# Loads of a Winograd-style 3x3 convolution: from casting transfers on GpSimd's queue to fp32 transfers on SyncE's

## The chip, the cores and the metric

One core of one Trainium2 chip runs the whole kernel. The time of a run is the device time of that core in microseconds (us). The profile is one further execution, recorded instruction by instruction; its span is counted from its first to its last recorded event and is a little shorter than the time of the same execution.

The engines are called by the names of the profile: PE (TensorE, matrix multiplications; PEld is its loading of weights), DVE (VectorE), ACT (ScalarE), POOL (GpSimd) and SP (SyncE, which only issues transfers). Engines run their own instruction lists in order and wait for one another by semaphores. Transfers (DMAs) are issued from the list of SP, ACT or POOL, each with a queue of its own (q1 for SP, q10 for ACT, q0 for POOL), and all queues are served by the same 16 DMA engines.

## The reference

```python
def setup_inputs():
    batch, c_in, h, w, c_out = 16, 64, 64, 64, 128
    return {
        "x": np.random.randn(batch, c_in, h, w).astype(np.float32),
        "weight": np.random.randn(c_out, c_in, 3, 3).astype(np.float32) * 0.1,
    }

def reference(x, weight):
    x_pad = np.pad(x, ((0, 0), (0, 0), (1, 1), (1, 1)), mode='constant')
    output = np.zeros((batch, c_out, h, w), dtype=np.float32)
    ...
    output[b, co] += weight[co, ci, kh, kw] * x_pad[b, ci, kh:kh+h, kw:kw+w]
    ...
```

A 3x3 convolution with zero padding over 16 images of 64 channels and 64x64 points, giving 128 channels. In fp32, 16.8 MB come in and 33.6 MB go out.

## The kernel before

**Tiling.** Two images make a pair: 2 x 64 channels fill the 128 partitions, so one pair is a tile of 128 x (64x64), 16 KB per partition in fp32, 2.10 MB in all. There are NP = 8 pairs. Each pair is worked in four blocks of RB = 8 pairs of output rows (16 output rows).

**The arithmetic.** Vertically the kernel computes two output rows at once with a scheme in the manner of Winograd's. For each pair p it keeps the input in fp16 (`xs[p]`) and the sums of neighbouring rows in fp16 (`ss[p]`, half as many rows, made by `sums`). A block has three groups of matmuls, each into two PSUM tiles `acc` (one for each image of the pair): U from `ss` with the middle weight row (6 matmuls), A from `xs` (12) and Bt from `xs` (12). ACT copies U out of PSUM into `ut`; DVE then adds A and `ut` into the even output rows and Bt and `ut` into the odd ones (the two `tensor_add` on `ots`). PSUM has 8 `acc` tiles (banks), `ut` has 4.

**Loads.** SP's queue brings the weights and then pairs 0, 1 and 2 in fp32 (`x0`, `x1`, `x2`) into homes of the output pool. Their fp16 form is made by ACT and POOL (`cast`): pair 0 partly ahead of the loop; pairs 1 and 2 by ACT in pieces of 16 rows, placed by the table `later` behind the U copies of blocks of pairs 0 and 1. Pairs 3 to 7 come through POOL's queue, and the transfer itself turns fp32 into fp16 (`load`), straight into `xs`; pairs 6 and 7 come in two halves. POOL also makes the row sums of pair p+1 during pair p.

**Stores.** Output homes hold one image each (16 KB per partition, `opool`, seven of them, three of which first hold x0 to x2). Image 0 of a pair is stored by SP at the pair's end, image 1 is put on the list `held` and stored by ACT behind the next U copies. The last pair is stored in halves, at blocks 1 and 3; image 0 of the first pair too.

**Order.** `keep` holds instructions of one engine in the order in which the program names them; everything else follows the program's order by tile dependencies.

Of the kernel before, what the change touches and what calls it, by code (L numbers as in the profile page):

```python
# [8 lines left out]
F32 = mybir.dt.float32  # L9
F16 = mybir.dt.float16  # L10
# [3 lines left out]
def kernel(  # L14
# [6 lines left out]
    nc = tc.nc  # L21
    B, CI, H, W = x.shape
    CO = weight.shape[0]
    assert H == 64 and W == 64 and CI == 64 and CO == 128 and B % 2 == 0
    NP = B // 2
    RB = 8

    keep = tc.keep_in_program_order
    x_rows = x.rearrange("b c h w -> (b c) h w")
    out_rows = out.rearrange("b co h w -> b co h w")  # L30
    w_flat = weight.rearrange("co ci kh kw -> co (ci kh kw)")

    const = ctx.enter_context(tc.tile_pool(name="const", bufs=1))
    psum = ctx.enter_context(tc.tile_pool(name="psum", bufs=8, space=bass.MemoryType.PSUM))
    xpool = ctx.enter_context(tc.tile_pool(name="xpool", bufs=8))
    opool = ctx.enter_context(tc.tile_pool(name="opool", bufs=7))
    spool = ctx.enter_context(tc.tile_pool(name="spool", bufs=3))
    upool = ctx.enter_context(tc.tile_pool(name="upool", bufs=4))

    w_raw = const.tile([CO, CI * 9], F32)  # L40
    nc.sync.dma_start(w_raw, w_flat)
    x0 = opool.tile([128, H, W], F32, tag="ot", name="x0")
    nc.sync.dma_start(x0, x_rows[0:128, :, :])
    x1 = opool.tile([128, H, W], F32, tag="ot", name="x1")
    nc.sync.dma_start(x1, x_rows[128:256, :, :])
    x2 = opool.tile([128, H, W], F32, tag="ot", name="x2")
    nc.sync.dma_start(x2, x_rows[256:384, :, :])
    raws = {1: x1, 2: x2}
    ident = const.tile([128, 128], F16)
    make_identity(nc, ident)  # L50
    w16 = const.tile([CO, CI * 9], F16)
    keep(nc.gpsimd.tensor_copy(w16, w_raw))  # L52

    xs = {p: xpool.tile([128, H, W], F16, tag="xs", name="xs") for p in range(3)}

    def load(p, rows):
        xs[p] = xpool.tile([128, H, W], F16, tag="xs", name="xs")
        for lo in range(0, H, rows):
            keep(
                nc.gpsimd.dma_start(  # L60
                    xs[p][:, lo : lo + rows, :],
                    x_rows[128 * p : 128 * p + 128, lo : lo + rows, :],
                )
            )

    ss = {}

    def sums(eng, p, src, lo, n):
        if p not in ss:
            ss[p] = spool.tile([128, H // 2, W], F16, tag="ss", name="ss")  # L70
        v = src.rearrange("p (j i) c -> p j i c", i=2)
        keep(
            eng.tensor_add(  # L73
                ss[p][:, lo : lo + n, :], v[:, lo : lo + n, 0, :], v[:, lo : lo + n, 1, :]
            )
        )
# [5 lines left out]
    def wrow(i):  # L82
        return Wt[:, i, :, :].rearrange("p t c -> p (t c)")

    wps = {}
    for kh in (1, 2, 0):
# [3 lines left out]
            for q in (0, 64):  # L90
                nc.tensor.matmul(wp[q : q + 64, k * CO : k * CO + CO], w16[:, t::9], ident)  # L91
        wps[kh] = wp[:, 0 : 3 * CO]
    blank = const.tile([128, 400], F32)
    keep(nc.vector.memset(blank, 0.0))  # L94
    warm = psum.tile([128, 512], F32, tag="acc", name="warm")
    for _ in range(3):
# [3 lines left out]
    keep(nc.vector.tensor_sub(wrow(G21), wps[2], wrow(G1)))  # L100
    keep(nc.vector.tensor_sub(wrow(G01), wps[0], wrow(G1)))  # L101

    def cast(copy, p, src, lo, hi):
        keep(copy(xs[p][:, lo:hi, :], src[:, lo:hi, :]))  # L104

    for lo in (RB, 2 * RB, 3 * RB):
        sums(nc.vector, 0, x0, lo, RB)
    cast(nc.scalar.copy, 0, x0, 0, 18)
    keep(nc.scalar.copy(wrow(G0), wps[0]))  # L109
    keep(nc.scalar.copy(wrow(G2), wps[2]))  # L110
    cast(nc.gpsimd.tensor_copy, 0, x0, 34, 50)
    cast(nc.gpsimd.tensor_copy, 0, x0, 50, 64)
    for p in (3, 4):
        load(p, H)
    later = {
        (0, 0): [(0, x0, 18, 34)],
        (0, 2): [(1, x1, 0, 16), (1, x1, 16, 32)],
        (0, 3): [(1, x1, 32, 48), (1, x1, 48, 64)],
    }
    later.update({(1, n): [(2, x2, 16 * n, 16 * n + 16)] for n in range(4)})  # L120

    held = []

    whole = {3: (0, 64)}
    halves = {1: (0, 32), 3: (32, 64)}
    cuts_of = [(halves, whole)] + [(whole, whole)] * (NP - 2) + [(halves, halves)]

    def store(eng, p, b2, ot, lo, hi):
        return eng.dma_start(
            out_rows[2 * p + b2, :, lo:hi, :],  # L130
            ot.rearrange("p j i c -> p (j i) c")[:, lo:hi, :],
        )

    for p in range(NP):
        if p + 1 < NP:
            for lo in (0, 16):
                sums(nc.gpsimd, p + 1, raws.get(p + 1, xs[p + 1]), lo, 16)
                if (p, lo) == (1, 16):
                    for q in range(5, NP):
                        load(q, H if q == 5 else H // 2)  # L140
        ots = [
            opool.tile([128, H // 2, 2, W], F32, tag="ot", name="ot") for _ in range(2)
        ]
        for blk in range(4):
            j0 = blk * RB

            def group(wi_rows):

                tiles = [
                    psum.tile([128, RB, W], F32, tag="acc", name="acc") for _ in range(2)  # L150
                ]
                n = 3 * len(wi_rows)
                i = 0
                for wi, off in wi_rows:
                    for kw in (1, 0, 2):
                        c_lo, c_hi = max(0, 1 - kw), min(W, W + 1 - kw)
                        for b2 in range(2):
                            p0 = 64 * b2
                            lo, hi = j0, j0 + RB
                            if off is None:  # L160
                                rhs = ss[p][p0 : p0 + 64, lo:hi, c_lo + kw - 1 : c_hi + kw - 1]
                            else:
                                while 2 * lo + off < 0:
                                    lo += 1
                                while 2 * (hi - 1) + off > H - 1:
                                    hi -= 1
                                first = 2 * lo + off
                                last = 2 * (hi - 1) + off
                                rhs = xs[p][
                                    p0 : p0 + 64,  # L170
                                    first : last + 1 : 2,
                                    c_lo + kw - 1 : c_hi + kw - 1,
                                ]
                            nc.tensor.matmul(  # L174
                                tiles[b2][:, lo - j0 : hi - j0, c_lo:c_hi],
                                Wt[p0 : p0 + 64, wi, kw, :],
                                rhs,
                                start=i == 0,
                                stop=i == n - 1,
                            )  # L180
                        i += 1
                return tiles

            U = group([(G1, None)])
            us = []
            for b2 in range(2):
                ut = upool.tile([128, RB, W], F32, tag="ut", name="ut")
                keep(nc.scalar.copy(ut, U[b2]))  # L188
                us.append(ut)
            while held and (p, blk) != (1, 0):  # L190
                keep(store(nc.scalar, *held.pop(0)))
            for piece in later.get((p, blk), ()):
                cast(nc.scalar.copy, *piece)
            A = group([(G21, 1), (G0, -1)])
            for b2 in range(2):
                nc.vector.tensor_add(ots[b2][:, j0 : j0 + RB, 0, :], A[b2], us[b2])  # L196
            Bt = group([(G01, 0), (G2, 2)])
            for b2 in range(2):
                nc.vector.tensor_add(ots[b2][:, j0 : j0 + RB, 1, :], Bt[b2], us[b2])  # L199
            if blk in cuts_of[p][0]:  # L200
                store(nc.sync, p, 0, ots[0], *cuts_of[p][0][blk])
            if blk in cuts_of[p][1]:
                held.append((p, 1, ots[1], *cuts_of[p][1][blk]))
    while held:
        keep(store(nc.scalar, *held.pop(0)))


# [28 lines left out]
```

## Time and profile before

| What | Value |
|---|---|
| Median of 3 runs | 126.22 us (126.04 to 126.24) |
| The profiled execution: its time / its span | 126.62 us / 124.8 us |
| PE busy | 108.0 us (86% of the span), last matmul about 112.3 |
| DVE busy | 84.5 us (68%) |
| ACT busy | 46.5 us (37%): 64 copies of U of 589 ns, 10 casts of about 1.07 us |
| POOL busy | 38.6 us (31%): 14 sums of 2.1 to 2.4 us, 7 issues of 574 ns |
| HBM | 17.07 MB read, 33.55 MB written, 406 GB/s over the span |
| Stores of one image (2 MB): issue to landing | median 19.0 us (ACT), 18.3 us (SP) |
| Half loads of pairs 6 and 7: issue to landing | median 51.2 us |

A matmul's busy time includes its pipeline, so a busy PE is not PE at its peak. "Busy" of DMA is the mean over its 16 engines. A landing is the time from an issue until the semaphore says that all of it has arrived. In rows of instruction groups, `out<-in` names the tiles, the number behind `x` counts instructions, and the bracket gives the idle time of the engine ahead of them and what ended it.

### The profile page before, as it was taken

What the parts mean: (1) busy time and instruction counts of PE and PEld (TensorE: products, weight loads), DVE (VectorE), ACT (ScalarE), POOL (GpSimd) and SP (SyncE); (2) the same over time, 40 slices, a digit from 0 to 9 for tenths busy, and PEclk for the clock granted to TensorE, in tenths of its full rate; (3) what the DMA queues carried; (4) which work ended last, traced back from release to release, by engine and by line L of the source; (5) the groups of instructions that cost most, each with busy time, mean ns of one, the idle gap of its engine ahead of it and who ended that gap; (6) DMA issues with size and microseconds to landing.
All of it is one profiled execution on the core that took longest, in us unless ns stands there. A gap on an engine that the chain in (4) does not pass through costs nothing.

```text
span 124.8 us, 2430 instructions
## 1 busy us (share of the span) xinstructions
PE 108.0 (86%) x984; PEld 49.8 (40%) x984; DVE 84.5 (68%) x135; ACT 46.5 (37%) x78; POOL 38.6 (31%) x30
## 2 busy tenths in 40 slices
PE   0699999999999999999999999999999999990000
PEld 0544444444444444444444444444444444430000
DVE  1019987877777887888777778777877787774000
ACT  4118559966653333333333333333333333330000
POOL 2219780799975001910240032004200510000000
PEclk9999999999999999999999999999999999999555
DMA  5899999999999999999999999999999999999991
GB/s 163 367 430 451 430 302 247 278 276 312 365 344 333 341 370 385 382 392 375 370 381 386 382 400 369 354 406 400 374 369 404 425 420 430 420 420 430 428 404 68
DMA packets 4330, 45.52 MB, mean 365 GB/s; under 512 B 480, under 2 KB 480, under 8 KB 1120
## 3 DMA queue, kind: packets, MB, share of 16 engines
q1 hardware_dynamic: 2016, 23.36, 45.0%
q10 hardware_dynamic: 1296, 16.78, 31.7%
q0 software_dynamic: 1008, 5.24, 20.8%
q8 instruction: 7, 0.11, 0.3%
q14 instruction: 3, 0.02, 0.0%
HBM read 17.07 MB, written 33.55 MB: 406 GB/s over the span
## 4 chain that ended last, share of the span: by engine, by line
PE 86%; DMA 2%; DVE 1%; issue 1%; POOL 1%; DVEq 0%
PE acc L174 81%; PE warm L97 3%; DMA w_raw<-in_weight_dram 2%; PE wp L91 1%; DVE ot L196 1%; POOL w L52 1%; DVEq L231 0%; DVE ot L199 0%; DVEq L196 0%
## 5 line engine op out<-in xcount | busy, mean ns | idle before, releaser
L174 PE MATMUL acc<-xs,Wt 64*128 64x504 f16 (+3 forms) x768 | 87.0, 374 | 0.0
L174 PEld LDWEIGHTS <-Wt 64*128 64x128 f16 x960 | 46.9, 95 | 56.2 <-issue 0.9
L188 ACT COPY ut<-acc 128x512 f32<-128x512 f32 x64 | 34.4, 589 | 56.9 <-issue 39.0
L196 DVE TENSOR_TENSOR ot<-acc,ut 128x512 f32<-128x512 f32 x64 | 41.2, 685 | 20.8 <-PE acc L174 18.4
L199 DVE TENSOR_TENSOR ot<-acc,ut 128x512 f32<-128x512 f32 x64 | 41.1, 683 | 0.0
L73 POOL TENSOR_TENSOR ss<-xs 128x1024 f16<-128x1024 f16 x10 | 21.1, 2130 | 49.3 <-DMA xs<-in_x_dram 49.3
L174 PE MATMUL acc<-ss,Wt 64*128 64x504 f16 (+1 forms) x192 | 26.0, 377 | 0.0
L104 ACT CAST xs<-x 128x1024 f16<-128x1024 f32 (+1 forms) x10 | 10.5, 1070 | 3.3 <-DMA x<-in_x_dram 3.3
L73 POOL TENSOR_TENSOR ss<-x 128x1024 f16<-128x1024 f32 x4 | 9.4, 2358 | 5.0 <-DMA x<-in_x_dram 5.0
L73 DVE TENSOR_TENSOR ss<-x 128x512 f16<-128x512 f32 x4 | 3.3, 868 | 7.5 <-DMA x<-in_x_dram 7.5
L91 PE MATMUL wp<-ident,w 128*64 128x128 f16 x18 | 1.3, 328 | 4.3 <-POOL w L52 4.3
L104 POOL CAST xs<-x 128x1024 f16<-128x1024 f32 (+1 forms) x2 | 3.0, 1518 | 4.5 <-DMA x<-in_x_dram 4.5
L97 PE MATMUL warm<-blank 128*128 128x400 f32 x6 | 4.2, 864 | 0.0
L60 POOL DMA_DIRECT2D xs<-in_x_dram x7 | 3.9, 574 | 0.0
L91 PEld LDWEIGHTS <-w 128*64 128x64 f16 x18 | 1.1, 210 | 4.3 <-POOL w L52 4.3
L97 PEld LDWEIGHTS warm<-blank 128*128 128x128 f32 x6 | 1.8, 326 | 1.4 <-issue 1.3
L98 ACT CAST Wt<-wp 128x384 f16<-128x384 f32 x1 | 0.5, 478 | 3.0 <-PE wp L91 3.0
L98 ACT ACT_TABLE_LOAD x1 | 1.3, 1283 | 0.7 <-PEq L220 0.7
L52 POOL CAST w<-w_raw 128x576 f16<-128x576 f32 x1 | 0.7, 663 | 2.3 <-DMA w_raw<-in_weight_dram 2.3
L94 DVE MEMSET blank<- 128x400 f32 x1 | 0.4, 392 | 0.9 <-PEq L220 0.9
L109 ACT CAST Wt<-wp 128x384 f16<-128x384 f32 x1 | 0.5, 478 | 0.5 <-DVE Wt L101 0.5
L100 DVE TENSOR_TENSOR Wt<-wp,Wt 128x384 f16<-128x384 f32 x1 | 0.6, 551 | 0.0
(8 smaller groups left out, 1.9 us busy)
## 6 DMA issues: line engine op xcount, KB each, us to landing
out_dram<-ot ACTq DMA_DIRECT2D x7, 2048.0 KB, 19.0
out_dram<-ot SPq DMA_DIRECT2D x6, 2048.0 KB, 18.3
x<-in_x_dram SPq DMA_DIRECT2D x3, 2048.0 KB, 12.0
out_dram<-ot SPq DMA_DIRECT2D x4, 1024.0 KB, 12.6
xs<-in_x_dram POOLq DMA_DIRECT2D x3, 1024.0 KB, 22.0
xs<-in_x_dram POOLq DMA_DIRECT2D x4, 512.0 KB, 51.2
out_dram<-ot ACTq DMA_DIRECT2D x2, 1024.0 KB, 11.1
w_raw<-in_weight_dram SPq DMA_DIRECT2D x1, 288.0 KB, 2.8
```

Of the source, the lines that this page charges most:

```text
L52: keep(nc.gpsimd.tensor_copy(w16, w_raw))
L60: nc.gpsimd.dma_start(xs[p][:, lo : lo + rows, :], x_rows[128 * p : 128 * p + 128, lo : lo + rows, :],)
L73: eng.tensor_add(ss[p][:, lo : lo + n, :], v[:, lo : lo + n, 0, :], v[:, lo : lo + n, 1, :])
L91: nc.tensor.matmul(wp[q : q + 64, k * CO : k * CO + CO], w16[:, t::9], ident)
L97: nc.tensor.matmul(warm[:, 0:400], blank[:, 0:128], blank)
L98: keep(nc.scalar.copy(wrow(G1), wps[1]))
L100: keep(nc.vector.tensor_sub(wrow(G21), wps[2], wrow(G1)))
L104: keep(copy(xs[p][:, lo:hi, :], src[:, lo:hi, :]))
L174: nc.tensor.matmul(tiles[b2][:, lo - j0 : hi - j0, c_lo:c_hi], Wt[p0 : p0 + 64, wi, kw, :], rhs, start=i == 0, stop=i == n - 1,)
L188: keep(nc.scalar.copy(ut, U[b2]))
L196: nc.vector.tensor_add(ots[b2][:, j0 : j0 + RB, 0, :], A[b2], us[b2])
L199: nc.vector.tensor_add(ots[b2][:, j0 : j0 + RB, 1, :], Bt[b2], us[b2])
```

## The change

- POOL issues no transfers any more. SP brings all eight pairs in fp32 (`load`), into four homes `raw0` to `raw3` (pair p in home p mod 4): pairs 0 to 3 at the start, pair 4 behind block (0,0) of the program in two halves, pair 5 behind block (0,3) whole, pair 6 behind (1,3) and pair 7 behind (2,3) in quarters of 16 rows. A load into a home that was used waits until the sums and casts of the pair before are done.
- ACT casts every pair from 1 on, one piece of 16 rows behind the U copies of each block of the pair before (`later`); the last piece of pair 7 moves to block (7,0). There are three `xs` homes instead of eight and two `ss` homes instead of three.
- Output homes hold a pair (32 KB per partition); there are three of them, pair p in home p mod 3.
- ACT issues all stores, through `held`, behind the next U copies: the two images of a pair one after the other; for the first and the last pair both images of half the rows in one transfer. SP stores nothing.
- The sums of the last pair are made in four pieces of 8 rows; `blank` takes a `ut` home.

```diff
-    xpool = ctx.enter_context(tc.tile_pool(name="xpool", bufs=8))
-    opool = ctx.enter_context(tc.tile_pool(name="opool", bufs=7))
-    spool = ctx.enter_context(tc.tile_pool(name="spool", bufs=3))
+    xpool = ctx.enter_context(tc.tile_pool(name="xpool", bufs=3))
+    rpool = ctx.enter_context(tc.tile_pool(name="rpool", bufs=1))
+    opool = ctx.enter_context(tc.tile_pool(name="opool", bufs=1))
+    spool = ctx.enter_context(tc.tile_pool(name="spool", bufs=2))
...
+    raws = {}
+    rows_of = {4: 32, 6: 16, 7: 16}
+
+    def load(p):
+        raws[p] = rpool.tile([128, H, W], F32, tag=f"raw{p % 4}", name="raw")
+        n = rows_of.get(p, H)
+        for lo in range(0, H, n):
+            keep(
+                nc.sync.dma_start(
+                    raws[p][:, lo : lo + n, :], x_rows[128 * p : 128 * p + 128, lo : lo + n, :]
+                )
+            )
+
+    for p in range(4):
+        load(p)
...
-    def load(p, rows):
-        xs[p] = xpool.tile([128, H, W], F16, tag="xs", name="xs")
-        for lo in range(0, H, rows):
-            keep(
-                nc.gpsimd.dma_start(
-                    xs[p][:, lo : lo + rows, :],
-                    x_rows[128 * p : 128 * p + 128, lo : lo + rows, :],
-                )
-            )
...
-    later.update({(1, n): [(2, x2, 16 * n, 16 * n + 16)] for n in range(4)})
+    later.update({(p, n): [(p + 1, *q4[n])] for p in range(1, NP - 1) for n in range(4)})
+    later[(NP - 1, 0)] = later.pop((NP - 2, 3))
+
+    def store(p, images, ot, lo, hi):
+
+        b = slice(images[0], images[-1] + 1)
+        dst = out_rows[2 * p : 2 * p + 2, :, lo:hi, :].rearrange("b co h w -> co b h w")
+        keep(
+            nc.scalar.dma_start(
+                dst[:, b, :, :], ot.rearrange("p b j i c -> p b (j i) c")[:, b, lo:hi, :]
+            )
+        )
...
-    whole = {3: (0, 64)}
-    halves = {1: (0, 32), 3: (32, 64)}
-    cuts_of = [(halves, whole)] + [(whole, whole)] * (NP - 2) + [(halves, halves)]
+    whole = {3: [((0,), 0, 64), ((1,), 0, 64)]}
+    halves = {1: [((0, 1), 0, 32)], 3: [((0, 1), 32, 64)]}
+    parts_of = [halves] + [whole] * (NP - 2) + [halves]
...
+            n = 8 if p + 1 == NP - 1 else 16
+            for lo in range(0, H // 2, n):
+                sums(nc.gpsimd, p + 1, raws[p + 1], lo, n)
+        ot = opool.tile([128, 2, H // 2, 2, W], F32, tag=f"out{p % 3}", name="ot")
...
-            while held and (p, blk) != (1, 0):
-                keep(store(nc.scalar, *held.pop(0)))
+            while held:
+                store(*held.pop(0))
...
-            if blk in cuts_of[p][0]:
-                store(nc.sync, p, 0, ots[0], *cuts_of[p][0][blk])
-            if blk in cuts_of[p][1]:
-                held.append((p, 1, ots[1], *cuts_of[p][1][blk]))
+            for part in parts_of[p].get(blk, ()):
+                held.append((p, part[0], ot, *part[1:]))
+            if (p, blk) == (0, 0):
+                load(4)
+            elif p < 3 and blk == 3:
+                load(p + 5)
```

## The prediction

> **What bounds the kernel now.** I read the page's busy rows first, then the chain, the DMA queues and the stretches by time, and last POOL's timeline.
>
> ```profile
> PE   0699999999999999999999999999999999990000
> DMA  5899999999999999999999999999999999999991
> PE acc L174 81%; PE warm L97 3%; DMA w_raw<-in_weight_dram 2%; PE wp L91 1%; DVE ot L196 1%; POOL w L52 1%; DVEq L231 0%; DVE ot L199 0%; DVEq L196 0%
> ...
> q1 hardware_dynamic: 2016, 23.36, 45.0%
> q10 hardware_dynamic: 1296, 16.78, 31.7%
> q0 software_dynamic: 1008, 5.24, 20.8%
> ```
>
> The chain names PE, whose matmuls run without a hole from 9.74 to about 112.3. But PE is idle in the last four slices, while the DMA row stays full almost to the end. The three queues' shares add up to 97.5%. DMA is the other bound: when PE is done, stores are still waiting in the queues.
>
> ```profile
> 108.00:111.00 3.00, 3.00 (x32) 1.36 (x28) 2.46 (x4) 1.07 (x2) 0.00 (x0) 1.00 1.01 426
> ...
> 115.00:115.50 0.50, 0.00 (x0) 0.00 (x0) 0.00 (x0) 0.00 (x0) 0.00 (x0) 0.71 1.04 442
> 115.50:116.00 0.50, 0.00 (x0) 0.00 (x0) 0.00 (x0) 0.00 (x0) 0.00 (x0) 0.50 0.89 377
> ...
> 122.00:124.80 2.80, 0.00 (x0) 0.00 (x0) 0.00 (x0) 0.00 (x0) 0.00 (x0) 0.50 0.13 53
> ```
>
> These are stretches; the last three columns are granted PE clock, DMA share and GB/s. With hardware queues alone DMA moves about 426 GB/s. The clock falls to half some 2.9 us after the last matmul. The last store is issued at 113.70 and lands 10.2 us later, at 123.9; the span ends 0.9 later.
>
> ```profile
> 61.66 2.12 POOL L73 TENSOR_TENSOR ss<-xs 128x1024 f16<-128x1024 f16 x1 [8.06 <-DMA xs<-in_x_dram]
> 73.69 2.12 POOL L73 TENSOR_TENSOR ss<-xs 128x1024 f16<-128x1024 f16 x1 [9.91 <-DMA xs<-in_x_dram]
> 86.04 2.13 POOL L73 TENSOR_TENSOR ss<-xs 128x1024 f16<-128x1024 f16 x1 [10.23 <-DMA xs<-in_x_dram]
> 98.21 2.12 POOL L73 TENSOR_TENSOR ss<-xs 128x1024 f16<-128x1024 f16 x1 [10.04 <-DMA xs<-in_x_dram]
> ```
>
> Each start is the landing of a half load of pairs 6 and 7 (1.05 MB read): one every 12.2 us. In the same 12.2 us each store queue moves one 2.10 MB image. The queues count 144 packets for every DMA of 128 rows (2016 is 14 DMAs, 1296 is 9, 1008 is 7): a packet is one row, and 16 are the semaphore's. So the three queues passed 128 packets each, of 8 KB, 16 KB and 16 KB: they take turns **by packet, not by byte**. This decides the case.
>
> **The change, part by part.** *Casting loads become fp32 loads.* The bytes at HBM stay (17.07 MB read, 33.55 written), and q0's 5.24 MB written were 10.49 MB read in 20.8% of 124.8 = 26.0 us, 404 GB/s. At 426 they take 24.6: a gain of 1.3 us of DMA time, bounds 0 (if mixing reads and writes is what slows them) to 1.6 (at 431 GB/s, the loads' rate in 6 to 9 us). I take 425 GB/s for all of the new kernel's DMA. POOL is rid of 7 issues (3.9 us), off the path.
>
> *ScalarE casts.* 20 more pieces of 128x1024 at 1.061 us, in blocks of 3.2 us that hold two copies (1.07 together): 2.1 of 3.2 us. Pair 1's blocks before already have this pattern, and PE had no hole there: nothing. POOL's sums from fp32 take 2358 ns instead of 2130, hidden while POOL is busy 31%. The eight-row pieces of the last sums (four for two) are hidden too.
>
> *Stores all on ACT.* An issue is 0.34 us, after the two copies of a block; ACT has 1 us of room. A hole between a pair's end and image 0's issue (it went out from SP 0.6 us earlier) costs nothing while DMA is backlogged. Homes: three pair homes ask that pair p-3's stores land before pair p's first add. By the sums below those of pair 0 land near 44 (wanted near 50) and those of pair 1 near 56 (wanted after 63): nothing, and up to 2 us if stores were that late.
>
> *The new wait.* The instruction lists of the two kernels show what the diff does not. Hardware DMAs take eight semaphores in turn in program order, and an issue waits until the DMA before it on its semaphore has landed. Before, these waits stood mostly between stores some 50 us apart. Now loads and stores share the turn. In the new list the semaphores are: load 6's quarters 2, 3, 4, 5; stores of pair 1 on 6 and 7 (7 is load 4's second half); load 7 on 0 to 3; **stores of pair 2 on 4 and 5, that is behind load 6's third and fourth quarters**. ACT's list has these waits on the two stores of block (3,0), and later no wait before its casts of those two quarters, so they are the ones waited for. Behind the waiting store on ACT stand the cast of pair 4's first quarter and the U copies of (3,1); DVE's adds wait for these, and PE for the banks.
>
> When does load 6 land? From about 19 us stores and loads alternate by packet. Pair 0's stores are 512 packets of 8 KB. Against them stand the rest of load 3 (some 120 of 16 KB), load 4 (256 of 8 KB) and load 5 (128 of 16 KB), about 500. So load 6 starts about where pair 1's stores start. These are 256 packets of 16 KB, load 6 is 512 of 4 KB. When pair 1's stores are through, half of load 6 is still to come, and ACT, stopped since 49.7 (before's issue of that store was at 49.67), has put nothing behind them. By then weights (0.29 MB), seven loads (14.68) and two pairs' stores (8.39) have to move, 23.36 MB, whatever their order:
>
> - first bytes 1.6 (the weights' issue is at 0.74, so 0.9 after it; the DMA share is 0.31 in 1 to 2 us) + 23.36/0.425 = 55.0, + 1.4 from last byte to semaphore (the weights, 0.29 MB, land at 3.56, x0 at 8.78: at 431 GB/s that leaves 1.3 and 1.6) = **58.0**. At the mean of before, 50.63 MB in 120.8 us = 419 GB/s, it is 58.8; at 431, 57.2.
> - ACT then casts (1.06) and copies U of (3,1) (1.07): 60.1. PE runs ahead in its 8 banks to the end of U of (3,2) and needs the copied bank for the next group, due at 49.7 - 1.9 + 2 x 3.2 + 0.65 = 54.9. **PE stands still 5.2 us** (4.4 to 6.0). DVE then works at 2.6 us a block against PE's 3.2 and catches up.
>
> Other shared semaphores: pair 1's image 1 waits for load 4, which by the same counting lands near 35 to 37, wanted at 36.9; PE's lead of 3 to 4 us covers it. Pair 4's and 5's stores (at 80 and 93) wait for load 7's quarters, landed by 79: nothing.
>
> *The end.* After 58 DMA has less to do than PE makes (4.19 MB per 12.8 us, 9.9 us at 425), so the queues empty before pair 6's stores are issued, at 100.9 + 5.2 = 106.1. From there: 0.9 to the first packet, 8.39 MB of pairs 6 and 7 at 425 = 19.7, 1.4 to land, 0.9 to the end: 129.0. The last half is issued at 113.7 + 5.2 = 118.9 and alone would end at 118.9 + 0.9 + 4.9 + 1.4 + 0.9 = 127.0, so DMA sets it. 129.0 - 124.8 = **+4.2 us**. Against the median, 126.22 + 4.2 = **130.4** (the profiled execution itself took 126.62, 1.8 above its span).
>
> PE's clock was seen to fall 2.9 us after its last matmul, and PE stands for 5.2. No row shows it rising again: bounds 0, and 3.2, a whole block at half speed. I take 0, since the sum has only one such hole, and keep 3.2 for the range.
>
> The Trainium skill, "TensorE: Matmul & The Clock Gate", section "Part 1: The HAM clock gate", says that the gate opens after about 3.4 us of sustained work in a free-running window of that length. By it some 1.7 us would be lost, and the sum would be 132.1.
>
> **The rivals.**
> *Equal bytes (faster).* If 4 KB rows of a hardware queue go several to a turn, load 6 gets half of the bandwidth: load 5 ends at 1.6 + 17.07 MB (weights, six loads, pair 0's stores)/0.425 = 41.8, load 6 then needs 9.9 us for 2.10 MB and lands at 53.1: 53.1 + 2.1 - 54.9 leaves a hole of 0.3, inside what PE's banks and DVE's lead blur. The end is 100.9 + 22.9 (the sum above) = 123.8, 1.0 less than now, so 125.2. It decides up to a landing at 53.8, where a hole of 1.0 gives all back. For it: rows of 4 KB were never seen on a hardware queue. Against it: POOL's halves, one packet each by turn. The skill, "DMA: Bandwidth & Descriptors", section "Queues, rings and completion order", says that an engine drains a whole packet, typically 9 to 17 descriptors, before it turns to the next ring; that speaks for this rival, but the packet counts here show one row to a packet.
> *The wait does not bite*, because it is satisfied some other way or load 6 is ahead: 125.2 again.
> *Half clock after the hole*: 130.4 plus 1.6 (half a block lost) to 3.2, about 132.2. For it the 0.71 and 0.50 above.
> *Mixed traffic is slow*: in 20 to 30 us before only 251 and 275 GB/s landed, with q0's packets counted at half of what they read. At q0's own 404 GB/s up to the landing, 23.36 MB take 57.8, the hole is 8.0 and the time 133.2.
>
> **How the numbers follow.** Forecast 0.58, half clock 0.15, slow mixing 0.08, equal bytes 0.12, wait without bite 0.05, and 0.02 between. The time is 130.4; without the faster cases its own range is 128.6 to 133. The range 125.8 to 133.6 takes in the slow mixing and leaves out most of the two fast cases and a half clock that costs a whole block on top of a late load. A difference of 0.2% (0.25 us) is what the runs can tell. Faster 0.16, same 0.03, slower 0.81.
>
> **What would show it.** Right: one PE hole near 55 to 60 with ACT idle from about 50 to 58 released by a DMA landing in raw; load 6's last quarters landing at 57 to 59; DMA share under 1 between 90 and 106, full from pair 6's stores on. Wrong: no PE hole; load 6 landed before 53; or a hole at another pair.

## The result, and the profile after

The changed kernel takes 135.18 us in the median of six runs (133.84 to 135.36), against 126.21 (126.04 to 126.36) for the kernel before beside it: a ratio of 1.0686, with an interval of 1.065 to 1.0722. The profiled execution took 133.97, its span is 132.2. On another chip four more runs of the same kernel gave 133.17 to 134.80. Medians are of all runs of a kernel, while ratios compare fast runs with fast runs and leave out those over 1.5% above the fastest of the same kernel. The steps below are measured on the profiled executions.

The busy rows of the page (the span in 40 slices of 3.3 us, tenths):

```profile
PE   0689999999999999701999999999999999997000
...
ACT  3138379666666661005856766666666636333000
...
PEclk9999999999999999995599999999999999999755
DMA  5999999999999999999999999799659946999993
```

Three things are new. ACT falls to 1, 0, 0 from 50 us on, and PE one slice later to 7, 0, 1 (53 to 63 us). The granted clock is 5 for two slices (59 to 66 us), in the second of which PE is busy again. DMA is full through the hole, and then has gaps (7, 6, 5, 4, 6) in which PE is busy all the time.

The instructions of ACT from 46 to 66 us in order of time (start, us, instruction; the bracket is the idle time before it and its releaser):

```profile
49.12 1.07 ACT L191 COPY ut<-acc 128x512 f32<-128x512 f32 x2 [1.14 <-issue]
58.92 1.85 ACTq L131 DMA_DIRECT2D out_dram<-ot  x2
60.81 1.04 ACT L108 CAST xs<-raw 128x1024 f16<-128x1024 f32 x1 [10.62 <-DMA raw<-in_x_dram]
61.77 1.07 ACT L191 COPY ut<-acc 128x512 f32<-128x512 f32 x2
```

ACT copies U of (3,0), and is then due to issue pair 2's two stores (L131). They go out at 58.92 and 60.44; in the kernel before at 49.07 (SP) and 49.67 (ACT). The releaser is the landing of a load in `raw`. The U copies of (3,1) stand behind. The chain of waits and the table of waits show who paid for it:

```profile
36.62 23.74 DMA raw<-in_x_dram
...
60.44 0.34 ACTq L131
...
60.81 0.04 ACT xs L108
...
61.77 0.59 ACT ut L191
62.35 0.04 issue
62.40 57.75 PE acc L177 x520
```

```profile
ACT xs L108 <- DMA raw<-in_x_dram: 14.0, 2, 10.6
...
DVE ot L199 <- ACT ut L191: 12.5, 6, 9.5
...
PE acc L177 <- ACT ut L191: 7.0, 1, 7.0
```

The chain (start, us, what) goes from load 6's last quarter, issued at 36.62 and landed at 60.36, over the second store's issue to the U copy, and from there to PE. In the table (total, times, longest) PE's wait is one piece of 7.0 us; DVE's longest is 9.5. The chain of before named neither a load in `raw` nor an `ut`.

Stretches of the same execution (PE, PEld, DVE, ACT, POOL busy, then clock, DMA share, GB/s):

```profile
55.00:56.00 1.00, 0.44 (x6) 0.09 (x1) 0.00 (x0) 0.00 (x0) 0.00 (x0) 1.00 0.99 418
56.00:58.00 2.00, 0.00 (x0) 0.00 (x0) 0.00 (x0) 0.00 (x0) 0.00 (x0) 1.00 1.00 410
58.00:60.00 2.00, 0.00 (x0) 0.00 (x0) 0.00 (x0) 0.00 (x0) 0.00 (x0) 0.80 1.02 365
60.00:62.00 2.00, 0.00 (x0) 0.00 (x0) 0.00 (x0) 1.19 (x2) 0.00 (x0) 0.50 1.00 260
...
64.00:66.00 2.00, 2.00 (x12) 1.02 (x10) 1.57 (x4) 1.70 (x3) 0.00 (x0) 0.50 1.00 426
66.00:68.00 2.00, 2.00 (x21) 1.12 (x18) 1.57 (x3) 0.31 (x1) 0.04 (x1) 0.99 1.04 436
95.00:100.00 5.00, 5.00 (x51) 3.13 (x49) 4.39 (x8) 2.80 (x5) 3.54 (x3) 1.00 0.51 213
100.00:105.00 5.00, 5.00 (x50) 2.90 (x47) 3.55 (x7) 3.67 (x6) 0.00 (x0) 1.00 1.04 446
105.00:110.00 5.00, 5.00 (x50) 3.07 (x48) 4.19 (x7) 1.80 (x4) 0.00 (x0) 1.00 0.45 187
110.00:120.00 10.00, 10.00 (x97) 5.86 (x94) 7.53 (x12) 4.61 (x8) 0.00 (x0) 1.00 0.99 419
```

PE stands still from 55.45 to 62.40. The clock falls at about 59.2 (0.80 is the mean of 58 to 60), 3.75 us after PE stopped, and is back at 66.0, 3.6 us after PE resumed: 12 matmuls in 64 to 66 against 21 in 66 to 68. At 95 to 100 and 105 to 110 DMA has nothing to do for half of the time. From pair 6's stores on (109.56) it is full to the end.

The trace also has the time at which each of the 16 DMA engines reports its part of a transfer. A semaphore is complete with the last of them:

```
                        8th engine   15th    16th (landing)
load 6, quarter 1          47.98     49.41    50.28
load 6, quarter 2          54.09     55.49    56.44
load 6, quarter 3          57.10     58.51    58.85
load 6, quarter 4          58.44     60.17    60.36
pair 1's second store      56.40     57.73    57.91
last store, after         130.41    131.05   131.35
last store, before        122.54    123.52   123.88
```

### The profile page after: what moved, and what is told of

It is laid out like the page before. It is cut to its first block, busy times and chain, and to the rows that moved or that the text cites. A ratio compares the mean times of both kernels' runs of the same rounds, so it can differ in the third digit from the quotient of the medians.

```text
span 132.2 us, 2462 instructions
## 1 busy us (share of the span) xinstructions
PE 109.6 (83%) x984; PEld 58.2 (44%) x984; DVE 84.5 (64%) x135; ACT 66.0 (50%) x98; POOL 37.4 (28%) x25
## 4 chain that ended last, share of the span: by engine, by line
PE 62%; DMA 24%; DVE 2%; issue 1%; SPq 1%; ACT 1%; DVEq 0%; ACTq 0%
PE acc L177 62%; DMA raw<-in_x_dram 24%; SPq L53 1%; ACT xs L108 1%; DVE ot L199 1%; DVE ss L75 1%; DVE ot L202 0%; DVEq L236 0%; ACT ut L191 0%; SPq L42 0%; ACTq L131 0%; ACTq L191 0%; DVEq L199 0%
## 5 line engine op out<-in xcount | busy, mean ns | idle before, releaser
L177 PE MATMUL acc<-xs,Wt 64*128 64x504 f16 (+3 forms) x768 | 93.3, 378 | 7.0 <-ACT ut L191 7.0
L177 PEld LDWEIGHTS <-Wt 64*128 64x128 f16 x960 | 55.5, 95 | 57.2 <-issue 10.2
L75 POOL TENSOR_TENSOR ss<-raw 128x1024 f16<-128x1024 f32 (+1 forms) x16 | 33.1, 2093 | 53.5 <-issue 41.6
L108 ACT CAST xs<-raw 128x1024 f16<-128x1024 f32 (+1 forms) x30 | 31.6, 1059 | 14.8 <-DMA raw<-in_x_dram 14.0
L177 PE MATMUL acc<-ss,Wt 64*128 64x512 f16 (+1 forms) x192 | 30.2, 377 | 0.6 <-DVE ss L75 0.6
L75 DVE TENSOR_TENSOR ss<-raw 128x512 f16<-128x512 f32 x4 | 3.3, 868 | 7.6 <-DMA raw<-in_x_dram 7.6
L108 POOL CAST xs<-raw 128x1024 f16<-128x1024 f32 (+1 forms) x2 | 3.0, 1519 | 4.6 <-DMA raw<-in_x_dram 4.6
L99 PE MATMUL warm<-blank 128*128 128x400 f32 x6 | 3.4, 731 | 0.0
L100 ACT CAST Wt<-wp 128x384 f16<-128x384 f32 x1 | 0.5, 479 | 3.0 <-PE wp L93 3.0
L113 ACT CAST Wt<-wp 128x384 f16<-128x384 f32 x1 | 0.5, 479 | 0.5 <-DVE Wt L103 0.5
L102 DVE TENSOR_TENSOR Wt<-wp,Wt 128x384 f16<-128x384 f32 x1 | 0.6, 550 | 0.0
L103 DVE TENSOR_TENSOR Wt<-wp,Wt 128x384 f16<-128x384 f32 x1 | 0.5, 548 | 0.0
L114 ACT CAST Wt<-wp 128x384 f16<-128x384 f32 x1 | 0.5, 484 | 0.0
## 6 DMA issues: line engine op xcount, KB each, us to landing
out_dram<-ot ACTq DMA_DIRECT2D x16, 2048.0 KB, 11.7
```

Of the source, the lines that this page charges most:

```text
L75: eng.tensor_add(ss[p][:, lo : lo + n, :], v[:, lo : lo + n, 0, :], v[:, lo : lo + n, 1, :])
L99: nc.tensor.matmul(warm[:, 0:400], blank[:, 0:128], blank)
L100: keep(nc.scalar.copy(wrow(G1), wps[1]))
L108: keep(copy(xs[p][:, lo:hi, :], raws[p][:, lo:hi, :]))
L177: nc.tensor.matmul(tiles[b2][:, lo - j0 : hi - j0, c_lo:c_hi], Wt[p0 : p0 + 64, wi, kw, :], rhs, start=i == 0, stop=i == n - 1,)
```

## The experiments

### Is it the wait on a shared semaphore?

**l7_whole** loads pair 7 in one transfer. All bytes and the order of the loads stay, but the turn of the eight semaphores is shorter by three, so pair 2's stores share with pair 0's second store and load 6's first quarter.

```diff
-    rows_of = {4: 32, 6: 16, 7: 16}
+    rows_of = {4: 32, 6: 16}
```

> Edit: load 7 in one transfer instead of four, so that the stores of pair 2 share their semaphores with pair 0's second store and load 6's first quarter, both landed by 51. Load 6 stays in quarters and stays late. Theory (ACT stops at a store that waits for load 6, and all behind it): no hole on PE near 55 to 62, store of pair 2 issued near 49.8, pair 6's stores near 101 and 22.6 us from there to the end: span 123.6 to 124.6, time 125 to 126, although load 6 lands still later than now (65 to 70), since stores of pair 2 now compete with it. Rival (DMA is slower as a whole in the new kernel, or ACT's doubled casts hold PE up): the hole or its loss stays, 131 or more.

Measured: 128.23 us, 1.0182 (1.0163 to 1.02). The stores go out at 49.19 and 49.68. The page's rows and the chain:

```profile
PE   0689999999999999999999999999999999950000
...
DMA  5899999999999999999999999999999999999960
```

```profile
9.53 101.61 PE acc L177 x948
```

All 948 matmuls of the loop stand in one piece, as before (101.39 there), and DMA has no gap. Load 6's last quarter lands at 67.72 there, 7.4 us later than in the changed kernel, and PE loses nothing by it. So the hole is the wait's. But the time is 2.3 us above before, where the run's expectation had 125 to 126 and the prediction's rivals without a hole 125.2.

**rows_whole** loads every pair in one transfer (rows of 16 KB throughout); **l6_whole** only pair 6, so that pair 2's second store still shares its semaphore with load 6.

```diff
-    rows_of = {4: 32, 6: 16, 7: 16}
+    rows_of = {}                     # rows_whole
+    rows_of = {4: 32, 7: 16}         # l6_whole
```

> Edit: every load in one transfer of 16-KB rows. Theory: no store waits for a late load, and a load has as many bytes to a turn as a store: load 6 lands at 52 to 55 instead of 60.4, no hole, time 124.8 to 126. Rival (turns go by byte, the size of the rows changes nothing): load 6 lands where it does with quarters and no stop. Rival (DMA slower as a whole): 131 or more.

> Edit: load 6 in one transfer of 16-KB rows, load 7 still in quarters. The second store of pair 2 still shares its semaphore with load 6. Theory (the lateness of load 6's small rows, taken by turns with 16-KB rows, makes the shared semaphore costly): load 6 lands at 48 to 51, as with all loads whole, the wait is met when it is asked, no hole, 127.5 to 128.5. Rival (sharing a semaphore between a load and a store costs in itself): a hole of several us stays, 131 or more.

Measured: 127.89 (1.015, 1.0134 to 1.0166) and 128.49 (1.018, 1.0147 to 1.0214), rows_whole about 2 us above its expectation and l6_whole within its own. Load 6, the same 2.10 MB, lands at 48.93 in rows_whole and at 53.16 in l6_whole in place of 60.36. l6_whole is the cleaner of the two: in rows_whole load 4 is whole too, and load 5 ahead of load 6 lands at 41.31 in place of 44.77. In the changed kernel, rows of both kinds start in every half us from 44 to 55.5. From 50 to 55 us the two queues passed about as many packets each (packets, MB, share of 16 engines):

```profile
q10 hardware_dynamic: 109, 1.65, 77.4%
q1 hardware_dynamic: 111, 0.40, 19.5%
```

So one row of 4 KB (q1) goes against one row of 16 KB (q10), and the small rows get a fifth of the bytes. Equal bytes falls (it had load 6 at 53.1).

In l6_whole the second store still waits for load 6, against the expectation (48 to 51, and no wait). It goes out at 53.23, just behind that landing and 3.7 us after the first (49.55), and ACT stands for 3.17 us. PE has no hole (ACT's instructions, and a line of the chain):

```profile
53.23 0.34 ACTq L131 DMA_DIRECT2D out_dram<-ot  x1
53.61 1.04 ACT L108 CAST xs<-raw 128x1024 f16<-128x1024 f32 x1 [3.17 <-DMA raw<-in_x_dram]
```

```profile
10.11 101.36 PE acc L177 x947
```

So a shared semaphore has a price only if the transfer ahead is later than PE's banks can bridge: 53.16 is early enough here, 60.36 is not, and PE stopped at 55.45.

**store_later** keeps loads, bytes and semaphores of the changed kernel and moves pair 2's two stores three blocks back in ACT's list. They still wait; but the casts and U copies of (3,0) to (3,2) are now ahead of them.

```diff
-            while held:
+            while held and (p, blk) not in ((3, 0), (3, 1), (3, 2)):
```

> Edit: the changed kernel, and pair 2's two stores stand three blocks later in ACT's list, behind the U copies of (3,3). Same queue, same semaphores, same small rows: the stores still wait for load 6's last quarters and go out at about the same time as now (59 to 61), but casts and U copies of (3,0) to (3,3) no longer stand behind them. Theory (the loss is what stands behind the wait on ACT): no hole at 55 to 62, at most 1 us of waiting for pair 2's output home at pair 5 (first add near 75, landing near 75), pair 6's stores at 100.5 to 102, time 127.5 to 129. Rival (the late stores of pair 2 themselves set the end, as when SP issued them): a hole of several us appears at pair 5 and the time stays over 131.

Measured: 129.16 (1.0246, 1.0227 to 1.0266), at the upper end of what was expected, span 127.7. ACT's instructions, and a line of the chain:

```profile
58.92 0.34 ACTq L131 DMA_DIRECT2D out_dram<-ot  x1
...
60.41 0.34 ACTq L131 DMA_DIRECT2D out_dram<-ot  x1
60.80 1.05 ACT L108 CAST xs<-raw 128x1024 f16<-128x1024 f32 x1 [0.92 <-DMA raw<-in_x_dram]
```

```profile
9.68 101.61 PE acc L177 x948
```

The stores leave as late as in the changed kernel (58.92 and 60.44 there), and PE has no hole. So the stores' delay by itself is not what costs most; what is queued behind them on ACT does: 132.2 - 127.7 = 4.5 us of span. The other 2.9 over before's 124.8 stay. In the landings of its last store the 8th engine is at 123.53 (before 122.54) and the 16th at 126.74 (before 123.88), so about 1.0 of the 2.9 is lost by the engines in general (1.2 by the 15th, at 124.76), and the rest by the last one alone. The 1.0 fits the thin traffic around 60 us: pair 2's first store, issued at 58.92, has its first packet at 63.04, and until then only load 7's 4-KB rows move.

**p2_on_sp** issues pair 2's stores from SP, where no cast or copy is behind them.

```diff
-            nc.scalar.dma_start(
+            (nc.sync if p == 2 else nc.scalar).dma_start(
```

> Edit: pair 2's two stores alone are issued by SP, with the same waits for load 6's third and fourth quarters. Theory (it is what stands behind the wait on ACT that costs, not the late store): SP waits until about 59 to 61, ACT and PE run on without a hole, DMA has load 7 to move meanwhile: time 125 to 126.5. Rival (the late store or DMA itself sets the end): 131 or more, with the end no earlier although PE has no hole.

Measured: 135.62 (1.0735, 1.065 to 1.082); its four times spread from 134.45 to 136.47, and the profile is of the longest, so only places are read from it. The chain, and three rows of the waits:

```profile
9.54 50.38 PE acc L177 x468
...
61.09 25.75 DMA out_dram<-ot
...
88.30 34.29 PE acc L177 x290
```

```profile
ACT ut L191 <- DVE ot L202: 14.3, 2, 12.2
...
DVE ot L199 <- DMA out_dram<-ot: 11.7, 1, 11.7
PE acc L177 <- DVE ot L199: 8.7, 1, 8.7
```

The hole at 55 is gone, but a longer one stands at pair 5 (PE idle to 87.70). Pair 2's stores, issued at 58.6 and 61.1, about as late as in the changed kernel, are on one queue behind load 7, so they take turns with pair 3's stores instead of going ahead of them, and land at 77.1 and 86.84; pair 5 needs their output home. The three pair homes, which the prediction had left at "nothing", set the time here: DVE wanted that home at about 75 (86.96 less its wait of 11.7), some 25 us after the stores were due.

### Is the half clock part of it?

**warm_fill36** and **warm_fill** put 36 and 45 matmuls that nobody uses just before U of (3,2), the last work that PE has ahead of the hole; U overwrites what they write. **after_again** is the changed kernel on the chip of warm_fill36.

```diff
+                if (p, blk, len(wi_rows)) == (3, 2, 1):
+                    for _ in range(36):
+                        nc.tensor.matmul(
+                            tiles[0].rearrange("p r c -> p (r c)")[:, 0 : 3 * CO],
+                            Wt[:, G1, 0, :],
+                            wrow(G1),
+                        )
```

> Edit: the changed kernel with 36 matmuls of 384 columns in the hole, 5.9 us, so that they end about 1 us before the hole does (with 45 they ended 1 us after it). Theory (half clock costs about 2 us): 1.7 to 2.3 less than the changed kernel on the same chip. Rival (it costs 1 or less, the rest of the loss is elsewhere): 0 to 1 less.

> Edit: 45 matmuls of 384 columns into the bank of U of block (3,2) before that group starts there, about 7 us of work that fills the hole; their results are overwritten. Theory (the fall of PE's clock in the hole costs 1.5 to 2.8 us on top of the hole): granted clock 1.0 throughout, ACT resumes as before near 61, pair 6's stores 1.7 earlier relative to the hole's end, time 132.5 to 133.7 with less spread between runs. Rival (half clock is hidden behind DVE's backlog): no change, 134 to 135.4.

> The changed kernel once more, to stand on one chip beside the others of this set. All theories: 133.8 to 135.4, load 6's last quarter near 60.4, a hole of about 7 on PE.

Measured: 133.73 (1.0602, 1.0554 to 1.065) with 36, 133.51 (1.0624, 1.0559 to 1.0688) with 45, and 133.98 (1.0619, 1.0561 to 1.0676) without. (The 133.73 and 133.98 are from one chip, the 133.51 from another.) PE's instructions and stretches of warm_fill36:

```profile
54.92 6.03 PE L158 MATMUL acc<-Wt 128*128 128x384 f16 x36
60.88 0.82 PE L184 MATMUL acc<-ss,Wt 64*128 64x512 f16 x6
62.77 3.24 PE L184 MATMUL acc<-xs,Wt 64*128 64x512 f16 x24 [1.07 <-ACT ut L198]
```

```profile
55.00:60.00 5.00, 5.00 (x32) 2.99 (x33) 0.00 (x0) 0.00 (x0) 0.00 (x0) 1.00 1.00 389
60.00:62.00 2.00, 1.70 (x12) 0.67 (x11) 0.00 (x0) 0.81 (x1) 0.00 (x0) 1.00 1.04 270
...
64.00:66.00 2.00, 2.00 (x22) 1.04 (x19) 2.00 (x5) 2.00 (x4) 0.00 (x0) 1.00 1.08 459
```

The fillers do not delay the work behind them (PE still waits 1.07 us after U), and the clock stays at 1.00: 22 matmuls in 64 to 66 in place of 12. From load 6's landing to the issue of pair 6's stores it is 60.74 to 108.40, 47.66 us; in after_again 60.34 to 109.37, 49.03, and in the first profile 49.20. The half clock so costs 1.4 to 1.5 us of PE's time. The total gains only 0.25 us, within what these runs scatter: the rival's 0 to 1, and not the 1.7 to 2.3 of the theory. Part of the reason can be seen. The last store's 8th engine is 1.0 earlier in warm_fill36 (129.24 against 130.22 in after_again), but its 16th is at 131.11, 0.9 after the 15th (130.18), while in after_again it is at 131.18, 0.3 after. Why the last engine is later there is open. With 45 the fillers end at 63.80, about 1 us after PE could have resumed, and give part back.

### Why is it still slower without the hole?

The versions without a hole should have been 1.0 us faster than before and were 1.6 to 2.4 slower (store_later, with its late stores, 3.1). These runs start from rows_whole (except before_act, which starts from the kernel before) and take away what could have caused it. The last three columns are the landings of the last store by engine.

| Run | Edit | Time | Ratio | 8th | 15th | 16th |
|---|---|---|---|---|---|---|
| before | | 126.21 | 1 | 122.54 | 123.52 | 123.88 |
| rows_whole | | 127.89 | 1.015 | 122.45 | 123.38 | 125.27 |
| before_act | image 0's stores also on ACT | 126.73 | 1.0055 (1.0038 to 1.0071) | 122.54 | 123.65 | 124.08 |
| halves_all | two half stores of both images for every pair | 127.88 | 1.0148 (1.0129 to 1.0167) | 122.74 | 123.61 | 125.18 |
| no_casts | ACT's casts of pairs 4 to 7 left out | 127.65 | 1.0126 (1.009 to 1.0162) | 122.29 | 123.65 | 124.83 |
| pool_loads | loads 4 to 7, still fp32, on POOL's queue | 127.67 | 1.0123 (1.0092 to 1.0155) | 122.37 | 122.62 | 124.64 |
| two_rings | image 0 of pairs 3 to 6 stored by SP | 127.74 | 1.0123 (1.0094 to 1.0151) | 123.24 | 124.20 | 124.81 |
| pool_ring | loads 4 to 7 on POOL's queue, all image 0's stored by SP | 134.48 | 1.0593 (1.0529 to 1.0656) | 129.20 | 129.66 | 130.13 |

```diff
-                store(nc.sync, p, 0, ots[0], *cuts_of[p][0][blk])       # before_act
+                held.append((p, 0, ots[0], *cuts_of[p][0][blk]))
...
-    parts_of = [halves] + [whole] * (NP - 2) + [halves]                # halves_all
+    parts_of = [halves] * NP
...
+        if p >= 4:                                                     # no_casts
+            xs[p] = xs[p - 3]
+            return
...
-                nc.sync.dma_start(                                     # pool_loads, pool_ring
+                (nc.sync if p < 4 else nc.gpsimd).dma_start(
...
-            nc.scalar.dma_start(
+            (nc.sync if images == (0,) and p >= 3 else nc.scalar).dma_start(   # two_rings
+            (nc.sync if images == (0,) else nc.scalar).dma_start(              # pool_ring
```

> Edit: the kernel before, with image 0's stores also issued by ACT (through the same list as image 1's); casting loads on POOL's queue stay. Theory (one ring for all stores lets one DMA engine fall behind, which costs the changed kernel without its hole 2 us): 127.5 to 128.5, the last landing 1.5 to 2.5 after the fifteenth. Rival (the fp32 loads, or other parts of the change, cost these 2 us): 125.9 to 126.5.

> Edit: the kernel with all loads whole, and every pair stored as the first and last are, both images of half the rows at a time (rows of 8 KB), all on ACT. Theory (the one engine's lag grows only while single images of 16-KB rows are stored from one ring): little lag, 125.3 to 126.5, less 0.9 of DMA time that 8-KB rows cost more (309 ns against 611 for 16 KB). Rival (the lag comes with one ring whatever the rows): 127.5 to 128.5.

> Edit: the kernel with all loads whole (127.9, no hole), and from pair 3 on image 0's store of the pairs with whole stores issued by SP. Theory (in that kernel one of the 16 DMA engines falls behind by 0.25 us an image while ACT's ring alone is served, and ends 2 us after the others, which is most of what it loses against before): with two rings the last store's landings lie closer together and the time falls to 125.5 to 126.5. Rival (the engine is slow whatever ring feeds it): the same 127.7 to 128.2.

> Edit: fp32 loads of pairs 4 to 7 whole on POOL's queue, image 0's whole stores on SP, the rest on ACT: before's three rings with ACT's casts in place of casting loads. Theory (what the change gains is about 1 us of DMA time, what it loses is the shared semaphores and the single store ring): 125 to 126.3. Rival (fp32 loads are no cheaper and lose elsewhere): 126.5 to 128.

> Edit: the kernel with all loads whole, without ACT's casts of pairs 4 to 7 (these pairs are computed from the fp16 form of pairs 1 to 3; loads, sums, matmuls and stores stay). Theory (ACT's reading of the fp32 homes while stores run slows one DMA engine): its lag over the fifteenth no longer grows after 75 us, 126.3 to 127. Rival (the lag has nothing to do with the casts): 127.7 to 128.1, the last landing 1.5 to 2.2 behind the fifteenth as before.

> Edit: the kernel with all loads whole, pairs 4 to 7 loaded in fp32 from POOL's queue, all stores still on ACT. Theory (loads on SP's ring, alone with the stores, leave one engine behind): 126.5 to 127, as in the kernel before with its stores all on ACT. Rival (fp32 instead of casting loads, from whatever queue): 127.6 to 128.3.

no_casts computes pairs 4 to 7 from the fp16 form of pairs 1 to 3, so its transfers are whole and ScalarE has 16 casts less.

pool_ring's four times lie between 132.97 and 136.79. None of these times bears out its theory: halves_all, no_casts, pool_loads and two_rings come out near their rivals, before_act just above its rival and pool_ring far above both.

What the table says: DMA's own time did fall. The packets of one engine take 122.3 us in sum before and 121.0 in rows_whole, the 1.3 us that the prediction had (121.5 in l7_whole; 122.9 in the changed kernel itself, where nothing is gained). But the end is set by the last of the 16 engines. Before it is 0.4 us behind the 15th; without casting loads it is 1.2 to 2.2 behind in all runs without a hole whose stores go on ACT alone (2.2 in l7_whole). Of the candidates, one store queue in place of two is worth 0.7 us (before_act) with the usual 0.4 of lag, so it isn't the lag: its last load lands at 71.33, and in the stores that follow alone on ACT's queue the lag stays at 0.1 to 0.5. Whole pairs against halves and SP's queue for the loads are excluded too: the lag stays at 1.6 and 2.0. Without ACT's casts it still reaches 1.8 (the store that lands at 110.10) and is 1.2 at the end, so the casts are at most a part of it. two_rings ends with 0.6, but it has a wait of 4.4 us for an output home at pair 5 (pair 2's second store lands at 79.68 there), which by itself lets a late engine catch up, and single stores on its two queues still lag by 1.7 (at 95.72) and 2.6 (at 112.58); so it settles nothing. pool_ring has such a wait of 8.4 us at pair 3 and shows only that. What makes one engine late is open. The loads are not moving any more when it happens: in rows_whole the last one lands at 63.68, and the lag grows after 69. What else the change brings into that stretch, output homes of a whole pair and POOL's sums from fp32, was not separated.

The lag grows with traffic and is small after a pause. In rows_whole it is 0.04 us in the store that lands at 69.18, 0.4 at 74.35, 1.6 at 94.99, and 1.7 to 1.9 from 105.31 on. In the changed kernel, whose queues run empty twice, it is 0.07 us at 115.91 and 0.3 at the end. But it can come back within one store: in warm_fill36 it is 0.07 at 101.95 and 1.4 at 108.54. So the hole's 7 us and this lag did not add up in the changed kernel.

## Why the prediction was wrong, and what of it held

The forecast was 130.4, with a range up to 133.6; the profiled execution took 133.97 and the median is 135.18. Which way the time would go, the wait and the place of the hole were right. Two steps of the sum failed: the landing of load 6 was dated 58.0 and came at 60.36, which made the hole 6.95 us in place of 5.2; and the half clock after the hole, put at nothing, took 1.4 to 1.5 us of PE's time.

- **The mechanism** came as forecast: pair 2's stores wait for load 6's last quarters, ACT stands from about 50, PE has one hole at 55, the queues run empty between 90 and 109 and are full from pair 6's stores on. l7_whole and store_later each take one link out, and the hole goes.
- **Turns by packet** held (rows_whole, l6_whole), and with it the byte count of the landing. In the Trainium skill, "DMA: Bandwidth & Descriptors", section "Queues, rings and completion order", a turn drains a packet of typically 9 to 17 descriptors. The trace differs, and decides: one row of 4 KB went against one row of 16 KB (about 110 packets of each queue from 50 to 55 us), and had several small rows gone to a turn, the prediction's count would have load 6 land at 53.1 and not at 60.36.
- **"= 58.0": mis-sized.** The step counts bytes at a mean rate and adds 1.4 us, taken from landings in which the engines lay close together (x0 in the kernel before: the 8th at 8.55, the 16th at 8.75). For the middle engine it is nearly right: the 8th reported at 58.44. The semaphore waits for the 16th, at 60.36, 1.9 later. The 15th is at 60.17, so it is not one engine alone; why they had drawn so far apart is open. The due time was 0.5 late as well (PE stopped at 55.45, not 54.9), so "PE stands still 5.2 us" became 6.95: 1.8 short.
- **Slow mixing** was not the reason, though its 133.2 comes near by luck. Only the stretch from 20 to 25 us was slow (344 GB/s); from 25 to 55 us, with loads and stores mixed, DMA moved 425 GB/s.
- **"I take 0" for the half clock: wrong, by 1.4 to 1.5 us of PE's time.** Its reason, that there is only one such hole, does not hold: one is enough. The rival had the mechanism and, with 1.6 to 3.2, nearly the size; its chance of 0.15 was too low. The Trainium skill's rule ("TensorE: Matmul & The Clock Gate", section "Part 1: The HAM clock gate") is that an idle window of about 3.4 us closes the gate and as long a busy one opens it. The trace agrees in the main: here it closed 3.75 us after PE stopped and opened 3.6 us after it resumed, and the stretches between two changes of the clock (6.83 us of half clock here, 10.24 in p2_on_sp) are 2 and 3 times 3.41 us. But at the end of the runs the clock fell from 2.2 us (warm_fill36) to 5.2 us (halves_all) after the last matmul, so the idle time that it takes varies.
- **"pair 6's stores ... at 106.1"** became 109.56. The hole is 1.8 of the 3.5, the clock 1.5. Without a hole these stores go out near 100.5 (100.41 in l7_whole, 100.56 in store_later) and not at 100.9 (-0.4). The remaining 0.6 is there in warm_fill36 too, at full clock, so it belongs to the restart and not to the clock; which instruction loses it is open.
- **The end** was right: 132.2 - 109.56 = 22.6, predicted 22.9. With the queues empty ahead of pair 6's stores, DMA's rate of 425 held and the 16th engine was not late. That part was luck: in warm_fill36, whose queues are empty there too, the same stretch took 23.5, with the 16th engine 0.9 late.
- **From span to time** the forecast stood 1.4 over its span, the profiled execution 1.8; and the first six runs' median is 1.2 above their profiled run. Why is open: three of the four longer runs have a lower mean clock (0.933 and 0.934 against 0.943 and 0.944), as a longer stretch of half clock would give, but the fourth has 0.948. With 1.8 + 1.5 + 0.6 - 0.4 - 0.3 + 0.4 = 3.6 the terms account for 133.97 - 130.4. They are dates of one profile and not separate costs: filling the hole took the clock's 1.5 out and gained only 0.25 us of the total. The range left the combination of a late load and a half clock out, and these two are not independent: it is the hole that makes the clock fall.
- **The rivals' 125.2** without a hole was too low by 2.4 to 3.3. The gain of 1.3 us of DMA time is there in the packets, and none of it at the end. Both the sum and its rivals took 16 engines as one.
- **Casts, issues and output homes at nothing** held for this order: no_casts is 0.2 us below rows_whole across two chips, too little to tell. The homes have little room, as p2_on_sp and pool_ring show.

No version of the fp32 loads that was run reaches the kernel before; the nearest, no_casts apart, are two_rings and pool_loads, both 1.0123.

## What to carry to other kernels

Before adding or cutting transfers, write down the turn of the DMA semaphores: an issue that meets a late transfer of another kind stops everything behind it on its engine, and a few transfers more or fewer elsewhere decide whether it does. Cutting a load into small rows makes it late when large rows compete, since each row is one turn (60.4 against 53.2 us here). Date a landing by the slowest of the 16 engines and not by the mean rate, and count the half clock that follows a long PE hole: holes of 5.5 us (pool_ring) and more had it here, holes of 1.1 and 1.4 us (warm_fill36, two_rings) did not, and none between was measured.

## What was not expected of the hardware

- One of the 16 engines ended 2.2 us after the fifteenth in a saturated run of large stores with no gap in the queues (l7_whole, 123.10 and 125.30), and 0.4 us after it in the kernel before.
- With load 7's 4-KB rows alone in the queues, DMA moved little while it counted as busy (two stretches of the changed kernel, columns as above):

```profile
60.00:61.00 1.00, 0.00 (x0) 0.00 (x0) 0.00 (x0) 0.18 (x1) 0.00 (x0) 0.50 1.06 307
61.00:62.00 1.00, 0.00 (x0) 0.00 (x0) 0.00 (x0) 1.00 (x2) 0.00 (x0) 0.50 0.94 213
```

  The shares (1.06, 0.94) are full and the GB/s (307, 213) are half to three quarters of the usual 425. A 4-KB packet takes 159 ns in the middle both here and beside stores, but a tenth of them take over 500 ns here.
- From 20 to 25 us, where the first stores begin beside load 3, 344 GB/s landed at a share of 0.98; load 3's 16-KB packets took 773 ns in the middle against 611 elsewhere. Casting transfers were no part of it, since this kernel has none.
- Pair 2's first store was issued at 58.92 in the changed kernel, and its first packet started at 63.06, 4.1 us later, although its queue was empty; for pair 6's first store (109.56) it was 0.85 us. Why is open.
